# Copying the sinks' columns on ScalarE, and finishing part of the last two rows on ScalarE and GpSimd

## The chip, the core and the metric

The kernel runs on one core of a Trainium2 chip. The core has a matrix engine (TensorE, PE in the profile), a vector engine (VectorE, DVE), a scalar engine (ScalarE, ACT), a general engine (GpSimd, POOL) and a queue that only issues DMAs (SyncE, SP). Each engine works through its own queue in order, and engines wait for each other on semaphores. A DMA that is issued from the queue of ACT or POOL stands in the same line as that engine's computing. The metric is the device time of one execution in microseconds; it was 950.13 us before the change (median of 3 runs, 949.94 to 950.27).

## What is computed

One decoder layer over 1024 tokens and 16 learned meta tokens, width 1024, all in float32:

```
u = rmsnorm(h, g_pre_mix);  q, k, v, xr, yr = split(u @ w_in)
attn = sliding_window_attention_with_sinks(q, k, v, sinks)     # window 128, 8 heads
rec  = gelu(yr) * rg_lru(conv(xr))                             # gated linear recurrence
h = h + rmsnorm(concat(attn, rec) @ w_out, g_post_mix)
f = square(relu(rmsnorm(h, g_pre_ffn) @ w_ff1)) @ w_ff2        # 1024 -> 4096 -> 1024
h = h + rmsnorm(f, g_post_ffn)
```

Two places matter here. In the attention, each head has a sink: a number that takes part in the softmax as one more key, with no value behind it.

```
m = max(max(s), sink);  p = exp(s - m);  denom = sum(p) + exp(sink - m)
```

At the very end, each row of `f` is divided by its root mean square, multiplied by `g_post_ffn`, and added to the residual `h`.

## The kernel before

**Matmuls.** A float32 product is made of three passes in the faster format (`mm3`, L125, L128, L129): each operand is split into a rounded part and a rest (L96 rounds on ACT, L99 takes the rest on DVE), and high by high, high by low and low by high are summed in PSUM. The feed-forward part saves products by sums of blocks, and stores and reloads some of them.

**Order of the work.** The program is written as one stream. A planner gives every instruction a place in its engine's queue, by priority and by a simulated time line of its own; on the chip the queues then run in that fixed order. `behind` (L106) adds an edge that only fixes an order, `lut` (L81) chains ACT's table functions. Buffers come from rings: tag "c" has 8 (L55), the banks of PSUM come in pairs by tag.

**Attention** (`scores`, L566, and `attend`, L620). For 4 pairs of heads and 2 halves of the sequence, `scores` fills two tiles `sn` from ring "c", [128, 4, 257]: two heads by two blocks of 128 queries, 256 keys each, and in column 256 the negated sink. The profile's names of tiles are those of their rings, so `sn` is "c", and its rows are found by line:

- L574, DVE: copies the sinks into column 256 of the four parts, a 128x4 copy; 16 of them in all;
- L590, PE: scores of one head, into a bank "s" of PSUM;
- L596, DVE: takes a bank "s", adds the mask, negates, writes columns 0 to 255, and keeps the minimum in `negm`;
- L604 (in the profile under L82), ACT: exp over columns up to 256, so with the sink, summed into `den`;
- L611, DVE: reciprocal of `den`; L615, POOL: adds the two halves of the keys' columns, 128x512; L616, DVE: divides.

In `attend` PE transposes (L627), ACT and DVE split the result (L96, L99), POOL cuts triangles out of it (L631), PE multiplies with the values (L641), and ACT and DVE take the result out of PSUM (L657, L658). Between them PE works on projections for the next heads and for the recurrence ("fills", with lower priority), which ACT and DVE take out of PSUM too (L117, L118, L451, L453).

**The end.** The second product of the feed-forward part goes in 56 steps. The last of them adds to rows 0 to 511, as four row blocks j = 0 to 3, one after another (L1500). For each, `finish_late` (L1409) adds the last product to the sum (L1415, in the profile under L1012, DVE), squares it with a running sum (L1416 calls L1380, ACT), multiplies by `g_post_ffn` (L1417, under L1012, DVE), takes the root (L1427, under L82, ACT) and the reciprocal `rs` (L1428, DVE). Block 3 comes in two parts of 256 columns for the first 512 columns' steps, so that its second part is short; the other 512 columns were summed earlier (`finish_half`). Then, for the two halves of a row block, columns 512 to 1023 first, one instruction on DVE scales by `rs` and adds the residual `h` (L1430, 128x512), and a DMA writes the half out: the first half from SP's queue, the second from ACT's (L1433). For blocks 0 to 2 these L1430 instructions are put in `held` and ordered behind an instruction of the next block (L1419, L1422), so that DVE takes the next block's sum out of PSUM first. For block 3 L1422 takes one entry of `held` for each of its two parts.

Of the kernel before, what the change touches and what calls it, by code (L numbers as in the profile page):

```python
# [11 lines left out]
AF = mybir.ActivationFunctionType  # L12
ALU = mybir.AluOpType
# [24 lines left out]
def hybrid_layer(  # L38
# [6 lines left out]
    nc = tc.nc  # L45
# [12 lines left out]
    def slot(tag, shape, dt=F32):  # L58
        uid[0] += 1
        return slab.tile(shape, dt, tag=tag, name=f"{tag}{uid[0]}", bufs=bufs[tag])  # L60
# [4 lines left out]
    def bank(tag, shape=(P, 512)):  # L65
        uid[0] += 1
        return ps.tile(list(shape), F32, tag=tag, name=f"ps_{tag}{uid[0]}")
# [13 lines left out]
    def lut(*args, **kwargs):  # L81
        ins = nc.scalar.activation(*args, **kwargs).ins  # L82
        if last_lut[0] is not None:
            tc.add_manual_dep(
                ins, last_lut[0],
                mybir.DependencyInfo(
                    mybir.DependencyClass.NoSync, mybir.DependencyReason.DATA
                ),
                reason="lut",
            )  # L90
        last_lut[0] = ins.name
        return ins
# [13 lines left out]
    def behind(name, *inss):  # L106
        for ins in inss:
            tc.add_manual_dep(
                ins, name,
                mybir.DependencyInfo(  # L110
                    mybir.DependencyClass.NoSync, mybir.DependencyReason.DATA
                ),
                reason="order",
            )
# [434 lines left out]
    for b in range(2):  # L549
        pv = bank("pt", (P, 4, P))  # L550
        for i in range(4):
            o = NMETA + (4 * b + i) * P
# [13 lines left out]
    def scores(j, half, q):  # L566

        g, pairs = j // 2, []
        for bp in range(2):
            sn = slot("c", [P, 4, 257])  # L570
            negm = small.tile([P, 4], F32, name="negm", tag="negm")
            den = small.tile([P, 4], F32, name="den", tag="den")
            rden = small.tile([P, 4], F32, name="rden", tag="rden")
            nc.vector.tensor_copy(  # L574
                sn.rearrange("p (h i) k -> p h i k", h=2)[:, :, :, 256],
                nsink[:, 2 * j : 2 * j + 2].to_broadcast([P, 2, 2]),
            )
            spans = [KEYS if 4 * half + 2 * bp + i else KEYS_0 for i in range(2)]
            if spans[0] is KEYS_0:
                nc.gpsimd.memset(  # L580
                    sn.rearrange("p (h i) k -> p h i k", h=2)[:, :, 0, 0 : P - NMETA], 0.0
                )
            for h in range(2):
                sp_ = bank("s", (P, 2, 256))
                for i, (w0, w1) in enumerate(spans):
                    b = 4 * half + 2 * bp + i
                    c = slice(b * P, (b + 1) * P)
                    o = NMETA + (b - 1) * P
                    for n, k_ in enumerate((khh, kl)):
                        nc.tensor.matmul(  # L590
                            sp_[:, i, w0:w1], q[h][:, c], k_[g][:, o + w0 : o + w1],
                            start=n == 0, stop=n == 1, skip_group_check=True,
                        )
                for i, (w0, w1) in enumerate(spans):
                    k = 2 * h + i
                    top = nc.vector.tensor_tensor_reduce(  # L596
                        out=sn[:, k, w0:w1], in0=sp_[:, i, w0:w1],
                        in1=mask[:, w0:w1], scale=-1.0,
                        scalar=nsink[:, 2 * j + h : 2 * j + h + 1],
                        op0=ALU.add, op1=ALU.min, accum_out=negm[:, k : k + 1],  # L600
                    ).ins
                    if (j, half, bp, k) == (3, 0, 0, 3):
                        behind(top.name, *held_back)
                    power = lut(  # L604
                        sn[:, k, w0:], sn[:, k, w0:], AF.Exp, scale=-1.0,
                        bias=negm[:, k : k + 1], accum_out=den[:, k : k + 1],
                    )
                    if j and half == bp == 0 and k in (0, 2):
                        behind(q_tail[j][0].name, power)
                        behind(q_tail[j][1].name, top)  # L610
            nc.vector.reciprocal(rden, den)  # L611


            one = sn[:, :, 0:P]
            nc.gpsimd.tensor_tensor(one, one, sn[:, :, P:256], op=ALU.add)  # L615
            nc.vector.tensor_tensor(one, one, rden.to_broadcast([P, 4, P]), op=ALU.mult)  # L616
            pairs.append(sn)
        return pairs
# [115 lines left out]
    for j in range(NPAIR):  # L734
        for half in range(2):
            if j % 2 == 0 and half == 0:
                at_pair(j // 2)
            sn = scores(j, half, qs[j])
            with deferred(0 if (j, half) in Q_SLOTS else FILL_LAG):
                next_fill()  # L740
            if (j, half) == (2, 1):
                graw = slot("raw", [P, NLRU, 2, HD])
                for s in range(2):
                    r = HALF[s]
                    for i, w in enumerate((w_x, w_a)):
                        nc.sync.dma_start(
                            graw[r, :, i ^ s, :], w[0, s::2].rearrange("n c d -> c n d")
                        )
                g_all = slot("b", [P, 2, NLRU, 2, HD], F32R)
                gw = g_all[:, 0], g_all[:, 1]  # L750
                with deferred(FILL_LAG):
                    split(*gw, graw)
            if prev is not None:
                attend(*prev)
            prev = (j, half, sn)
# [6 lines left out]
    for s in range(2):  # L762
        for i in range(2):
            nc.vector.tensor_scalar(
                gbias[HALF[i ^ s], s, :], prm[HALF[s], :, 6 - i], 0.5, None,
                op0=ALU.mult,
# [244 lines left out]
    def combine(dst, x0, x1, op):  # L1011
        return nc.vector.tensor_tensor(dst, x0, x1, op=op).ins  # L1012
# [363 lines left out]
    COLS = (slice(0, 512), slice(512, 1024))  # L1376

    def squares(sq, src, n):
        p_ = small.tile([P, 1], F32, name=f"sq{n}", tag=f"sq{n}")
        nc.scalar.activation(sq, src, AF.Square, scale=RMS_SC, accum_out=p_)  # L1380
        return p_
# [11 lines left out]
    halves, held = {}, []  # L1393
# [15 lines left out]
    def finish_late(j, y, parts):  # L1409

        h, o, ssq = halves[j]
        acc = facc["0", j]
        for k, c in enumerate(parts):
            yield k
            last = combine(acc[:, c], y[k], acc[:, c], ALU.add).name  # L1415
            part = squares(y[k], acc[:, c], k)  # L1416
            scaled = combine(o[:, c], acc[:, c], gffn_b[:, c], ALU.mult)  # L1417
            if len(parts) == 1:
                behind(last, *held)  # L1419
                held.clear()  # L1420
            else:
                behind(scaled.name, held.pop(0))  # L1422
            if k < len(parts) - 1:
                nc.vector.tensor_tensor(ssq, ssq, part, op=ALU.add)
        root = small.tile([P, 1], F32, name="root", tag="root")
        rs = small.tile([P, 1], F32, name="rs", tag="rs")
        lut(root, part, AF.Sqrt, bias=ssq)  # L1427
        nc.vector.reciprocal(rs, root)  # L1428
        for c, eng in zip(COLS[::-1], (nc.sync, nc.scalar)):
            held.append(nc.vector.scalar_tensor_tensor(  # L1430
                o[:, c], o[:, c], rs, h[:, c], op0=ALU.mult, op1=ALU.add
            ).ins)
            eng.dma_start(out[j * P : (j + 1) * P, c], o[:, c])  # L1433

    written = set()
# [64 lines left out]
    for j in range(4):  # L1500
        parts = col_parts(6, j)
        for k in finish_late(j, accs[j], parts):
            for n in sorted(ready):
                step_mm(accs[j][k], j, steps[n][1], ready[n], parts[k])
# [31 lines left out]
```

## Time and profile before

| | |
|---|---|
| median of 3 runs | 950.13 us (949.94 to 950.27) |
| the profiled execution's own time | 949.87 us |
| its span, first to last instruction | 947.9 us |
| granted TensorE clock | 0.998 |
| ACT busy | 500.2 us (53%) |
| DVE busy | 679.3 us (72%) |
| POOL busy | 154.7 us (16%) |
| HBM | 115.70 MB read, 23.07 MB written |

How to read the profile's rows. A row of the time line has the start in us from the span's start, the duration in us, engine, line, operation, output and inputs by their rings' names, shape, and a count if several neighbours are merged; in brackets stands the idle time just ahead of it on its engine, and what ended that. Starts and durations of neighbours on one engine overlap a little. A row of the waits names who waited for whom, the sum in us, how often, and the longest. A row of the windows has the stretch, its length, then busy time and count of instructions for PE, its weight loads, DVE, ACT and POOL, then the granted clock, the share of the DMA engines and GB/s. A matmul's shown duration is longer than the distance to the next one, because matmuls are pipelined.

### The profile page before, as it was taken

To read this page: it belongs to the slowest core of one execution; us is meant where nothing else is said; L and a number is where in the kernel's file an instruction comes from. 1 tells how busy PE (TensorE), PEld (TensorE's weight loads), DVE (VectorE), ACT (ScalarE), POOL (GpSimd) and SP (SyncE) were. 2 spreads that over 40 slices of the span, in tenths; PEclk is the share of its full clock that TensorE was granted. 3 is DMA by queue.
4 is the path that set the end of the run, shared out by engine and by line. 5 is a ranking of instruction groups with operands and counts; after the bars stand their busy time and mean duration, and the time that the engine had idled before them with its cause. 6 is when DMAs were issued, how large, how long until landed. Compare 5 with 4: busy or idle time off the path is not lost.

```text
span 947.9 us, 12401 instructions
## 1 busy us (share of the span) xinstructions
PE 938.9 (99%) x4661; PEld 784.7 (83%) x4661; DVE 679.3 (72%) x963; ACT 500.2 (53%) x826; POOL 154.7 (16%) x198
## 2 busy tenths in 40 slices
PE   9999999999999999999999999999999999999997
PEld 8999899878888888888888888888888888888886
DVE  6679898878966786665654566576667676769884
ACT  7556686579345554443655565564533343445451
POOL 2116674600020100000110001101121000003020
PEclk9999999999999999999999999999999999999999
DMA  8221001212245466685655567645677665567412
GB/s 286 53 52 39 23 27 31 89 45 90 80 165 178 134 222 200 201 278 155 222 173 193 156 199 229 204 150 151 155 180 179 181 216 201 175 202 156 115 64 89
DMA packets 85466, 140.62 MB, mean 148 GB/s; under 512 B 5752, under 2 KB 48776, under 8 KB 85408
## 3 DMA queue, kind: packets, MB, share of 16 engines
q1 hardware_dynamic: 74944, 108.39, 35.3%
q0 software_dynamic: 9600, 29.36, 12.1%
q10 hardware_dynamic: 864, 2.10, 0.6%
q8 instruction: 36, 0.59, 0.2%
q14 instruction: 22, 0.18, 0.1%
HBM read 115.70 MB, written 23.07 MB: 146 GB/s over the span
## 4 chain that ended last, share of the span: by engine, by line
PE 97%; DVE 2%; ACT 0%; POOL 0%; issue 0%; DMA 0%; DVEq 0%; ACTq 0%
PE ps_acc L125 12%; PE ps_acc L128 11%; PE ps_acc L129 11%; PE ps_pt L129 7%; PE ps_pt L128 7%; PE ps_pt L125 7%; PE ps_s L125 6%; PE ps_s L129 6%; PE ps_s L128 6%; PE ps_o L125 5%; PE ps_o L129 5%; PE ps_o L128 5%; PE ps_o L641 1%; PE ps_s L590 1%; PE ps_o L986 1%; PE ps_acc L278 1%
## 5 line engine op out<-in xcount | busy, mean ns | idle before, releaser
L96 ACT CAST ws<-raw 128x1024 fp32r<-128x1024 f32 (+1 forms) x64 | 65.4, 1023 | 96.6 <-PE ps_o L128 47.9
L99 DVE TENSOR_TENSOR ws<-raw,ws 128x1024 fp32r<-128x1024 f32 (+1 forms) x65 | 79.0, 1215 | 40.4 <-ACT ws L96 40.4
L125 PE MATMUL ps_acc<-a,ws 128*128 128x256 f32 (+2 forms) x256 | 85.8, 335 | 0.0
L128 PE MATMUL ps_acc<-a,ws 128*128 128x256 f32 (+2 forms) x256 | 84.9, 332 | 0.0
L129 PE MATMUL ps_acc<-a,ws 128*128 128x256 f32 (+2 forms) x256 | 84.7, 332 | 0.0
L96 ACT CAST ws<-e 128x1024 fp32r<-128x1024 f32 x41 | 42.9, 1047 | 65.4 <-PE ps_o L128 38.1
L99 DVE TENSOR_TENSOR b<-b,b 128x1024 fp32r<-128x1024 f32 (+2 forms) x48 | 57.6, 1199 | 27.6 <-PE ps_o L128 22.4
L99 DVE TENSOR_TENSOR ws<-e,ws 128x1024 fp32r<-128x1024 f32 x41 | 50.1, 1223 | 27.1 <-ACT ws L96 27.1
L96 ACT CAST b<-b 128x1024 fp32r<-128x1024 f32 (+2 forms) x48 | 49.4, 1030 | 37.7 <-DVE b L1012 34.6
L631 POOL TENSOR_SCALAR_AFFINE_SELECT c<-c 128x512 fp32r<-128x512 f32 x64 | 54.2, 872 | 30.9 <-ACT c L96 27.2
L178 POOL TENSOR_TENSOR rs<-ms,half_pow 128x1 f32<-128x1 f32 x26 | 19.3, 749 | 204.5 <-DVE ms L174 203.4
L125 PEld LDWEIGHTS ps_acc<-a,ws 128*128 128x128 f32 x256 | 48.2, 188 | 5.4 <-issue 0.6
L129 PEld LDWEIGHTS ps_acc<-a,ws 128*128 128x128 f32 x256 | 48.2, 188 | 4.8
L128 PEld LDWEIGHTS ps_acc<-a,ws 128*128 128x128 f32 x256 | 48.2, 188 | 4.3 <-issue 0.2
L125 PE MATMUL ps_acc<-ws,b 128*128 128x512 f32 (+1 forms) x120 | 46.4, 386 | 0.0
L129 PE MATMUL ps_acc<-ws,b 128*128 128x512 f32 (+1 forms) x120 | 46.2, 385 | 0.0
L128 PE MATMUL ps_acc<-ws,b 128*128 128x512 f32 (+1 forms) x120 | 46.2, 385 | 0.0
L129 PE MATMUL ps_pt<-ws,b 128*128 128x512 f32 x112 | 44.1, 394 | 0.0
L128 PE MATMUL ps_pt<-ws,b 128*128 128x512 f32 x112 | 44.1, 394 | 0.0
L125 PE MATMUL ps_pt<-ws,b 128*128 128x512 f32 x112 | 43.9, 394 | 0.0
L125 PE MATMUL ps_s<-ws,b 128*128 128x512 f32 x110 | 43.3, 395 | 0.0
L128 PE MATMUL ps_s<-ws,b 128*128 128x512 f32 x110 | 43.3, 394 | 0.0
(427 smaller groups left out, 2715.1 us busy)
## 6 DMA issues: line engine op xcount, KB each, us to landing
raw<-in_w_ff_dram SPq DMA_DIRECT2D x51, 512.0 KB, 4.3
e<-in_w_ff_dram SPq DMA_DIRECT2D x33, 512.0 KB, 3.9
m<-in_w_ff_dram SPq DMA_DIRECT2D x16, 512.0 KB, 4.5
raw<-in_w_in_dram SPq DMA_DIRECT2D x12, 512.0 KB, 4.9
d<-in_w_ff_dram SPq DMA_DIRECT2D x12, 512.0 KB, 4.0
s_dram<-d POOLq DMA_DIRECT2D x12, 512.0 KB, 4.0
raw<-in_w_ff_dram POOLq DMA_DIRECT2D x10, 512.0 KB, 5.7
e<-in_w_ff_dram POOLq DMA_DIRECT2D x9, 512.0 KB, 5.7
```

Source lines behind the costliest of these rows:

```text
L96: nc.scalar.copy(hi, src)
L99: low = nc.vector.tensor_tensor(lo, src, f32(hi), op=ALU.subtract).ins
L125: ins = nc.tensor.matmul(dst, lh, rh, start=start, stop=False, skip_group_check=True).ins
L128: nc.tensor.matmul(dst, lh, rl, start=False, stop=False, skip_group_check=True)
L129: last_mm[0] = nc.tensor.matmul(dst, ll, rh, start=False, stop=stop, skip_group_check=True).ins.name
L178: last_pow[0] = nc.gpsimd.tensor_tensor(rs[:n], ms[:n], half_pow[:n], op=ALU.pow).ins.name
L278: last_mm[0] = nc.tensor.matmul(acc[:, :n], w[k // 2][:, kc, :], u[kc][k % 2][:, t0 : t0 + n], start=k == 0 and kc == 0, stop=k == last an ...
L590: nc.tensor.matmul(sp_[:, i, w0:w1], q[h][:, c], k_[g][:, o + w0 : o + w1], start=n == 0, stop=n == 1, skip_group_check=True,)
L631: nc.gpsimd.affine_select(out=m[:, :, side, :], in_=f32(m)[:, :, 1, :], pattern=[[0, 4], [-sign, P]], compare_op=op, fill=0.0, base=0, cha ...
L641: ins = nc.tensor.matmul(po[:, :, oc : oc + size], v, m[:, :, pc : pc + size], start=first and k == 0, stop=last and k == 1, skip_group_ch ...
L986: nc.tensor.transpose(pt[:, i, :], xn[:, kc * P : (kc + 1) * P], ident)
```

## The change

Three edits:

```diff
@@ scores
-            nc.vector.tensor_copy(
+            nc.scalar.copy(
                 sn.rearrange("p (h i) k -> p h i k", h=2)[:, :, :, 256],
                 nsink[:, 2 * j : 2 * j + 2].to_broadcast([P, 2, 2]),
             )
@@ finish_late
             if len(parts) == 1:
                 behind(last, *held)
                 held.clear()
-            else:
+            elif held:
                 behind(scaled.name, held.pop(0))
...
         nc.vector.reciprocal(rs, root)
+        shared = {2: 512, 3: 256}.get(j)
         for c, eng in zip(COLS[::-1], (nc.sync, nc.scalar)):
-            held.append(nc.vector.scalar_tensor_tensor(
-                o[:, c], o[:, c], rs, h[:, c], op0=ALU.mult, op1=ALU.add
-            ).ins)
+            mine = c
+            if shared and c is COLS[0]:
+                s_ = slice(0, shared)
+                nc.scalar.activation(o[:, s_], o[:, s_], AF.Copy, scale=rs)
+                nc.gpsimd.tensor_tensor(o[:, s_], o[:, s_], h[:, s_], op=ALU.add)
+                mine = slice(shared, 512)
+            if mine.start < mine.stop:
+                held.append(nc.vector.scalar_tensor_tensor(
+                    o[:, mine], o[:, mine], rs, h[:, mine], op0=ALU.mult, op1=ALU.add
+                ).ins)
             eng.dma_start(out[j * P : (j + 1) * P, c], o[:, c])
```

The 16 copies of the sinks' columns go from DVE to ACT. Of row block 2, columns 0 to 511 are scaled by ACT and added to the residual by POOL, with nothing left of that half for DVE. Of row block 3, columns 0 to 255 go the same way, and DVE keeps columns 256 to 511. Columns 512 to 1023 of both blocks stay with DVE. `held` then has one entry of block 2, so the second part of block 3 finds it empty. The DMA of the first 512 columns stays on ACT's queue; of block 2 it now waits for POOL, and of block 3 for POOL and DVE.

## The prediction

> **What bounds the kernel now.** I read the page first, then PE's waits, then the stretches of the two places that the change touches.
>
> ```profile
> PE 938.9 (99%) x4661; PEld 784.7 (83%) x4661; DVE 679.3 (72%) x963; ACT 500.2 (53%) x826; POOL 154.7 (16%) x198
> ...
> PE 97%; DVE 2%; ACT 0%; POOL 0%; issue 0%; DMA 0%; DVEq 0%; ACTq 0%
> ```
>
> PE is busy nearly always, and the chain that ended last is 97% PE. So time is saved in two ways only: a gap in PE is closed, or the work behind the last matmul gets shorter. PE's waits, all of them:
>
> ```profile
> PE ps_acc L299 <- POOL b L293: 1.6, 1, 1.6
> PE ps_s L590 <- DVE negm L596: 0.7, 1, 0.7
> PE ps_o L348 <- DVE d L254: 0.3, 1, 0.3
> ```
>
> The first and the third lie in the kernel's first 10 us, and the change doesn't touch them. The second is a score matmul (L590) that waits until DVE has emptied its bank. It is the only gap of the stage with the sinks, and of everything after it. The windows say how full the engines are there:
>
> ```profile
> 61.00:104.00 43.00, 42.26 (x295) 39.10 (x295) 37.37 (x103) 30.95 (x91) 24.99 (x27) 1.00 0.13 38
> 104.00:157.00 53.00, 53.00 (x353) 48.70 (x352) 49.44 (x111) 34.40 (x96) 30.82 (x35) 1.00 0.13 35
> ...
> 941.66:947.93 6.27, 0.00 (x0) 0.00 (x0) 3.00 (x6) 0.80 (x3) 0.00 (x0) 0.72 0.44 167
> ```
>
> DVE is the fullest engine beside PE (37.37 of 43.00 us, 49.44 of 53.00), ACT has a third free. The last row is the end: no matmul, DVE works for 3.00 us, then the last write lands and the program closes.
>
> **The sinks' copies.** What the 16 copies cost now, and where the gap comes from (line 574 as a whole, then DVE, POOL, PE and ACT around the gap):
>
> ```profile
> L574 DVE COPY c<-nsink x16: 155/168/1286, 26.1 to 155.8; 128x4 f32<-128x4 f32 x16
> ...
> 96.09 1.35 DVE L574 COPY c<-nsink 128x4 f32<-128x4 f32 x2
> 97.36 0.17 DVE L611 RECIPROCAL rden<-den 128x4 f32<-128x4 f32 x1
> 97.56 0.43 DVE L658 TENSOR_TENSOR e<-ps_o,e 64x256 f32<-64x256 f32 x1
> 98.02 0.48 DVE L596 CUSTOM_DVE_ANT_0 c<-ps_s,m,nsink 128x256 f32<-128x256 f32 x1
> ...
> 96.12 1.30 POOL L615 TENSOR_TENSOR c<-c 128x512 f32<-128x512 f32 x1
> ...
> 97.83 0.28 PE L128 MATMUL ps_acc<-a,ws 128*128 128x256 f32 x1
> 97.95 0.28 PE L129 MATMUL ps_acc<-a,ws 128*128 128x256 f32 x1
> 98.97 0.51 PE L590 MATMUL ps_s<-b,b 128*128 128x256 f32 x2 [0.74 <-DVE negm L596]
> ...
> 95.98 0.76 ACT L657 COPY e<-ps_o 64x256 f32<-64x256 f32 x2
> 98.02 0.62 ACT L96 CAST b<-e 128x512 fp32r<-128x512 f32 x1 [1.28 <-DVE e L658]
> ```
>
> A copy takes 0.168 us in the median, but one took 1.286. It ended at 97.44, just when POOL's addition that began at 96.12 was over (97.42): the two did not run side by side, DVE stood still for it. Behind it in DVE's queue are L611, L658 and then the two L596 that empty the bank; PE's next score matmul starts at 98.97, 1.02 us after its predecessor, where neighbours are 0.12 apart (97.83, 97.95). So the gap costs **0.90 us**. (The 0.74 in brackets is less, since a matmul's shown end is late.)
>
> Without the copies L611 can start at 96.1. L658 needs ACT's first copy of 95.98, half of 0.76, so it starts at 96.4 and ends at 96.8; the two L596, 0.41 apart, end near 97.7. PE wants the bank at 98.07. The gap is closed with 0.35 us to spare. If ACT puts both new copies ahead of L657, 0.3 to 0.4 us go, and it still closes or nearly so.
>
> What ACT pays: a 128x4 copy is not in the trace for ACT. Nearest are the 128x64 casts and the longer 64x256 copies (0.38):
>
> ```profile
> L96 ACT CAST vm<-ps_o x2: 213/216/220, 59.3 to 59.8; 128x64 fp32r<-128x64 f32 x2
> ```
>
> I take 0.2 us, 16 times 3.2 us, from nothing to 16 x 0.38 = 6.1. In both windows together ACT has 96.00 - 65.35 = 30.65 us free, and this hides it. If it were not hidden, a copy would delay an exp by 0.2 us, and PE only where a bank is already late. The DVE time that comes free beyond this gap buys nothing: PE has no other gap there. Term: **-0.90 us**.
>
> **The end.** DVE, then ACT:
>
> ```profile
> 939.97 0.16 DVE L1428 RECIPROCAL rs<-root 128x1 f32<-128x1 f32 x1
> ...
> 940.49 0.43 DVE L1012 TENSOR_TENSOR a<-a,a 128x256 f32<-128x256 f32 x1
> 940.83 0.75 DVE L1430 SCALAR_TENSOR_TENSOR a<-a,rs,d 128x512 f32<-128x512 f32 x1
> 941.49 0.15 DVE L1424 TENSOR_TENSOR late<-late,sq 128x1 f32<-128x1 f32 x1
> 941.70 0.42 DVE L1012 TENSOR_TENSOR a<-ps_acc,a 128x256 f32<-128x256 f32 x1
> 942.15 0.43 DVE L1012 TENSOR_TENSOR a<-a,a 128x256 f32<-128x256 f32 x1
> 942.50 0.74 DVE L1430 SCALAR_TENSOR_TENSOR a<-a,rs,d 128x512 f32<-128x512 f32 x1
> 943.16 0.15 DVE L1428 RECIPROCAL rs<-root 128x1 f32<-128x1 f32 x1
> 943.35 1.42 DVE L1430 SCALAR_TENSOR_TENSOR a<-a,rs,d 128x512 f32<-128x512 f32 x2
> ...
> 942.15 0.39 ACT L1380 ACTIVATE ps_acc<-a 128x256 f32<-128x256 f32 x1 [1.16 <-DVE a L1012]
> 942.48 0.19 ACT L1380 ACTIVATION_READ_ACCUMULATOR ps_acc<-a 128x1 f32 x1
> 942.70 0.29 ACT L82 ACTIVATE root<-sq,late 128x1 f32<-128x1 f32 x1
> 943.27 1.86 ACTq L1433 DMA_DIRECT2D out_dram<-a  x2
> ```
>
> Now DVE's last instruction ends at 944.77, and the write behind it closes the kernel. Block 2's L1430 at 942.50 goes away; the root is there at 942.99, so the last reciprocal could start at 943.02 in place of 943.16, 0.14 sooner. Then half of the last L1430 goes: 0.43 in place of 0.75.
>
> Against it stands POOL, which must read the same memory as DVE:
>
> ```profile
> 85.92 1.53 DVE L99 TENSOR_TENSOR ws<-raw,ws 128x1024 fp32r<-128x1024 f32 x1
> ...
> 86.34 2.26 POOL L615 TENSOR_TENSOR c<-c 128x512 f32<-128x512 f32 x1
> ...
> 915.36 5.67 POOL L1405 TENSOR_SCALAR late<-late 128x1 f32<-128x1 f32 x1 [7.55 <-ACT a L1402]
> ...
> 915.12 1.22 DVE L99 TENSOR_TENSOR ws<-raw,ws 128x1024 fp32r<-128x1024 f32 x1
> ...
> 919.73 1.22 DVE L99 TENSOR_TENSOR a<-e,a 128x1024 fp32r<-128x1024 f32 x1
> ```
>
> L615 took 2.26 us in place of 1.30 when it met an L99, and ended 1.15 us after that (87.45 to 88.60). A 128x1 instruction of POOL took 5.67 us while DVE ran six with two inputs in SBUF, back to back from 915.12 to 920.95. So the two exclude each other, and a row of DVE instructions can keep POOL out. In the Trainium skill, SBUF — State Buffer, section Who interferes with whom, says the same: a VectorE instruction with two SBUF inputs and a GpSimd instruction that reads SBUF share an interface, and the one that starts second is blocked for the whole of the other. By that rule the end comes out 0.45 us later than if both ran freely, and the rows agree with it.
>
> With exclusion: ACT scales block 2's half from 940.16. The 0.60 us of a 128x512 square is 0.39 at 256 columns, and with a scale from memory 256 columns cost 0.48 (12 of L117):
>
> ```profile
> L117 ACT ACTIVATE a<-ps_o,gcol x12: 468/481/496, 9.5 to 52.2; 128x256 fp32r<-128x256 f32 x9, 128x272 fp32r<-128x272 f32 x3
> ...
> 938.17 0.60 ACT L1380 ACTIVATE ps_pt<-a 128x512 f32<-128x512 f32 x1 [3.04 <-DVE a L1012]
> ```
>
> That gives 0.69 for 512 columns, until 940.85. POOL is kept out by DVE (940.49 to 941.64), then runs its 1.15 beside the sum from PSUM, until 942.8. DVE's product of 942.15 has two inputs in SBUF and waits for that; some 0.1 of its 0.43 are over by then, so it ends at 943.1, and the reciprocal starts near 943.05, 0.1 sooner than now. The last L1430 of columns 512 to 1023 starts 0.19 behind (as 943.16 to 943.35), so 943.24 to 943.99. ACT scales 256 columns until 943.75, and POOL is ready at 943.85 but shut out until 943.99. POOL's 256 columns are not in the trace: between half of 1.15 and 1.30; I take 0.65, since a 128x1 instruction shows a fixed part. With DVE's 0.35 to 0.43 one after the other, in either order, the end is 943.99 + 0.65 + 0.4 = 945.04, against 944.77: about **+0.25 us**. With the dearest POOL (1.30) it is +0.9; with no exclusion the chain is 943.02 + 0.19 + 0.48 + 0.1 + 0.75 = 944.55, **-0.2**.
>
> **Sum.** -0.90 + 0.25 = -0.65 us. The profiled execution took 949.87 (span 947.9, 2 us around it), so 949.2; the median of the runs lies 0.26 above that one, so I forecast **949.5**. A change under 0.2% (1.9 us) is about what a measurement of this kernel can tell from no change.
>
> **Rivals.**
>
> *POOL and DVE run side by side at the end.* -0.90 - 0.2 = -1.1: 949.0. The L615 and L1405 rows speak against it. 10%.
>
> *ACT's queue is late at the end.* Block 2's second DMA stands in ACT's queue and now waits for POOL (942.8). If the planner thinks POOL is done before 942.15 and puts it ahead of the last squares, these wait until 942.8 plus the 0.35 us of an issue (942.85 to 943.2) in place of 942.15, 1.05 later, and root, reciprocal and end follow. Sum 0.25 + 1.05 - 0.90 = +0.4: 950.5. In the trace block 2's DMA stands behind the root (943.27 after 942.70), but there it was ready later, too. 15%.
>
> *The gap only moves.* Another instruction of DVE meets POOL, or L658 is late because the copies stand ahead of L657, and PE loses the same 0.9 elsewhere: +0.25: 950.4. That no other gap is there now speaks against it. 10%.
>
> *Slower: the copies hold ACT.* On ACT a copy that must wait for its buffer of ring "c" (eight, still read by POOL and PE) holds the exps and PSUM evictions queued behind it, and PE runs out of banks. On DVE, nearly always late itself, this wait was over each time; ACT, with a third free, would reach it sooner. A late bank costs about what the one of now costs, 0.9. It decides from three such places: 3 x 0.9 - 0.65 = +2.05; with four it is +2.95: 953.1. Twelve of the 16 copies lie behind 60 us, in seven or so places. ACT's idle stretches (1.28 ahead of 98.02) speak against it. 15%.
>
> *Faster by more than 1.9 us.* PE has nothing left to give but the start; the end would have to lose a microsecond as well, out of the 3.1 between 941.66 and 944.77. Only a planner's order that changes elsewhere could do it. 5%.
>
> My forecast has 45%. Within 0.2% are it and the first three rivals, 80%; slower 15%, faster 5%. The range takes in 949.0 to 950.5 and the bounds of POOL's price and of ACT's copies: 948.6 to 951.2.
>
> **What would show it.** PE's wait L590 <- DVE is gone from the list, and PE's last matmul ends near 940.76. L574 stands on ACT, 16 at 0.2 us. POOL's two additions at the end take 1.3 to 1.9 and 0.8 to 1.2 us from their starts, because of waits; DVE's product on the last part ends together with POOL's first addition plus 0.3. The last matmul to the last ACT DMA issue grows from 3.1 to 3.4 us. I am wrong if PE shows new waits between 60 and 157 us, or ACT's squares wait behind a DMA.

## The result, and the profile after

The changed kernel takes **951.98 us** (median of 11 runs, 951.82 to 954.08; the kernel before on the same chip 950.13). The ratio (of the means) is 1.0023, with a 95% interval of 1.0015 to 1.0031. So the change makes the kernel slower, by 1.85 us in the medians, where 0.6 us faster was forecast, and the time lies above the forecast's range of 948.6 to 951.2. The profiled execution took 951.91 us, with a span of 950.2 us in place of 947.9.

The span is 2.3 us longer, and the traces say in which two places. TensorE's last matmul ends at 942.89 in place of 941.66, 1.23 later, where 0.90 earlier was forecast. From there to the issue of the last DMA (the last L1441 row below; L1430 of before is L1438 in the changed file, L1433 is L1441, and L1434 and L1435 are the new scaling on ACT and addition on POOL) it is now 4.20 us (942.89 to 947.09), against 3.14 before (941.66 to 944.80): 1.06 more, where 0.25 more was forecast. The last issue of before, by itself:

```profile
944.80 0.34 ACTq L1433 DMA_DIRECT2D out_dram<-a  x1
```

First TensorE's waits in the changed kernel, all of them (who waited for whom, sum in us, how often, the longest), and line 574 as a whole:

```profile
PE ps_acc L299 <- POOL b L293: 1.6, 1, 1.6
PE ps_acc L125 <- ACT d L705: 1.6, 1, 1.6
PE ps_o L158 <- DMA vmt<-in_g_pre_ffn_dram: 0.6, 1, 0.6
PE ps_o L348 <- DVE d L254: 0.3, 1, 0.3
...
L574 ACT COPY c<-nsink x16: 183/197/208, 27.5 to 144.4; 128x4 f32<-128x4 f32 x16
```

The wait of L590 for DVE is gone, as forecast. The copies stand on ACT with 0.197 us each. One of the sixteen, at 31.86, came behind 0.43 us in which ACT waited for DVE's L228; ahead of the others the view shows no wait. In place of L590's wait stands a new row: a matmul of L125 waits 1.6 us for ACT's L705. That is a projection for the recurrence, outside the stage that the change touches. The stage with the sinks is now full:

```profile
61.00:104.00 43.00, 43.00 (x299) 39.99 (x299) 37.69 (x106) 32.75 (x98) 26.07 (x28) 1.00 0.13 38
104.00:157.00 53.00, 53.00 (x357) 48.75 (x356) 47.62 (x102) 35.54 (x103) 30.86 (x36) 1.00 0.10 27
```

PE is busy for 43.00 of 43.00 us in place of 42.26, and does 299 matmuls in the first stretch where it did 295. So the gap was closed, and the time was gained there. Counted by the nth matmul to start, the changed kernel is 0.13 us behind the kernel before at 80 us (from the waits of the start), 0.77 ahead at 99 us, so that 0.90 was gained, and 1.33 ahead at 180 us.

**Lost at 180 us.** The time line there, of before (PE, ACT and DVE), and ahead of it the row of who waited for L705's copies, from the view of that line:

```profile
  PEld ps_acc L125: 0.6, 2
...
180.14 0.40 PE L129 MATMUL ps_acc<-a,ws 128*128 128x512 f32 x1
180.52 0.50 PE L125 MATMUL ps_acc<-a,ws 128*128 128x512 f32 x1
...
179.88 0.59 ACT L705 COPY d<-ps_acc 128x512 f32<-128x512 f32 x1 [0.89 <-DVE b L673]
...
178.52 1.33 DVE L673 SCALAR_TENSOR_TENSOR b<-d,prm,b 128x1037 f32<-128x1037 f32 x1
```

And the same instructions in the changed kernel:

```profile
178.81 0.40 PE L129 MATMUL ps_acc<-a,ws 128*128 128x512 f32 x1
180.78 0.50 PE L125 MATMUL ps_acc<-a,ws 128*128 128x512 f32 x1 [1.57 <-ACT d L705]
...
180.15 0.58 ACT L705 COPY d<-ps_acc 128x512 f32<-128x512 f32 x1 [1.53 <-DVE b L673]
...
178.71 1.35 DVE L673 SCALAR_TENSOR_TENSOR b<-d,prm,b 128x1037 f32<-128x1037 f32 x1
```

L705 takes the first projection of the gates' branch out of PSUM into a tile of ring "d". Its tile is the one that the convolution's last step (L673, on DVE) still reads, so L705 waits for that step, and the next L125 waits for L705 to empty the bank. In the kernel before, L673 ended at 179.85, L705 at 180.47, and L125 began at 180.52. That chain was just in time: PE lost 0.15 us there. It had no row among PE's waits: only the spacing of the matmuls (0.38 in place of 0.23) and the 0.6 us that two of PE's weight loads waited show it. In the changed kernel PE is there 1.33 us sooner (178.81 against 180.14), while DVE's convolution is 0.2 us later. So PE stands for 1.57 us, and the lead is gone: by the same count PE is 0.29 behind at 182 us.

**Lost at 195 us.** Here the order of PE's queue is another one. The first gates (L790) are 18 matmuls of 64 rows. Before, they ran together, two at a time, a pair every 0.16 us (first two rows, last two of 18, and the matmul behind them):

```profile
193.64 0.43 PE L790 MATMUL ps_s<-b,b 64*128 64x348 f32 x1
193.65 0.43 PE L790 MATMUL ps_pt<-b,b 64*128 64x348 f32 x1
...
195.02 0.32 PE L790 MATMUL ps_pt<-b,b 64*128 64x344 f32 x1
195.03 0.32 PE L790 MATMUL ps_o<-b,b 64*128 64x344 f32 x1
195.27 0.50 PE L125 MATMUL ps_acc<-a,ws 128*128 128x512 f32 x1
```

In the changed kernel the planner put three matmuls of a projection in between (five L790, one, ten, two, three L790):

```profile
193.28 0.42 PE L790 MATMUL ps_s<-b,b 64*128 64x348 f32 x1
...
193.71 0.32 PE L790 MATMUL ps_pt<-b,b 64*128 64x344 f32 x1
193.96 0.49 PE L125 MATMUL ps_acc<-a,ws 128*128 128x512 f32 x1
194.38 0.42 PE L790 MATMUL ps_s<-b,b 64*128 64x348 f32 x1
...
195.53 0.50 PE L128 MATMUL ps_acc<-a,ws 128*128 128x512 f32 x1
...
196.19 0.73 PE L790 MATMUL ps_o<-b,b 64*128 64x344 f32 x3
196.85 0.50 PE L125 MATMUL ps_acc<-a,ws 128*128 128x512 f32 x1
```

Before, the 18 take 1.63 us (193.64 to 195.27). After, they take 3.57 (193.28 to 196.85), of which the three others are worth 3 x 0.23 = 0.69 at their usual spacing. So 1.25 us are lost where halves stand without a partner and where the form changes (how the loss divides between the two isn't shown), with no gap that a view of waits would list. By the same count the changed kernel is 0.20 behind at 193 us, 1.56 behind at 198, and 1.23 behind at its last matmul.

**Lost at the end.** The changed kernel's end, DVE first, then POOL and ACT:

```profile
942.09 0.74 DVE L1438 SCALAR_TENSOR_TENSOR a<-a,rs,d 128x512 f32<-128x512 f32 x1
942.75 1.22 DVE L1424 TENSOR_TENSOR late<-late,sq 128x1 f32<-128x1 f32 x1
943.89 0.41 DVE L1012 TENSOR_TENSOR a<-ps_acc,a 128x256 f32<-128x256 f32 x1
...
945.21 0.16 DVE L1428 RECIPROCAL rs<-root 128x1 f32<-128x1 f32 x1 [0.44 <-ACT root L82]
945.40 1.61 DVE L1438 SCALAR_TENSOR_TENSOR a<-a,rs,d 128x512 f32<-128x512 f32 x2
...
942.25 1.71 POOL L1435 TENSOR_TENSOR a<-a,d 128x512 f32<-128x512 f32 x1 [19.94 <-ACT a L1434]
945.99 0.75 POOL L1435 TENSOR_TENSOR a<-a,d 128x256 f32<-128x256 f32 x1 [2.04 <-ACT a L1434]
...
941.44 0.72 ACT L1434 ACTIVATE a<-a,rs 128x512 f32<-128x512 f32 x1 [0.90 <-DVE rs L1428]
...
947.09 0.34 ACTq L1441 DMA_DIRECT2D out_dram<-a  x1
```

POOL's addition for block 2 became ready at 942.25, while DVE ran L1438. By the durations it got in when that ended: from 942.83 to its own end at 943.96 are 1.13 us, about the 1.15 that the prediction's L615 took once DVE was done. The next instruction in DVE's queue was the small addition L1424, 128x1: it took 1.22 us in place of 0.15, and ended with POOL's. Behind it in the queue stood the sum out of PSUM (L1012), for which PE had been done since 942.89. It started at 943.89, 1.00 later, where the kernel before took 0.04. Of the 1.06 us, 0.96 are lost here. From this sum to the last reciprocal it is 0.14 less than before (1.32 in place of 1.46), and from there to the last DMA's issue 0.24 more (1.88 in place of 1.64).

### The profile page after: what moved, and what is told of

It reads as the page before. It is cut to its first block, busy times and chain, and to the rows that moved or that the text cites. A ratio compares the mean times of both kernels' runs of the same rounds, so it can differ in the third digit from the quotient of the medians.

```text
span 950.2 us, 12413 instructions
## 1 busy us (share of the span) xinstructions
PE 938.8 (99%) x4661; PEld 785.3 (83%) x4661; DVE 676.5 (71%) x946; ACT 503.2 (53%) x844; POOL 154.4 (16%) x200
## 4 chain that ended last, share of the span: by engine, by line
PE 94%; DVE 4%; ACT 1%; POOL 0%; DMA 0%; issue 0%; DVEq 0%; SPq 0%; ACTq 0%; POOLq 0%
PE ps_acc L125 11%; PE ps_acc L128 11%; PE ps_acc L129 11%; PE ps_pt L129 7%; PE ps_pt L128 7%; PE ps_pt L125 7%; PE ps_s L125 6%; PE ps_s L129 6%; PE ps_s L128 6%; PE ps_o L125 5%; PE ps_o L129 5%; PE ps_o L128 5%; PE ps_o L641 1%; PE ps_s L590 1%; PE ps_o L986 1%; PE ps_acc L278 1%
## 5 line engine op out<-in xcount | busy, mean ns | idle before, releaser
L125 PE MATMUL ps_acc<-a,ws 128*128 128x256 f32 (+2 forms) x256 | 85.9, 336 | 1.6 <-ACT d L705 1.6
L128 PE MATMUL ps_acc<-a,ws 128*128 128x256 f32 (+2 forms) x256 | 85.6, 334 | 0.0
L631 POOL TENSOR_SCALAR_AFFINE_SELECT c<-c 128x512 fp32r<-128x512 f32 x64 | 51.4, 826 | 32.2 <-ACT c L96 23.9
L125 PEld LDWEIGHTS ps_acc<-a,ws 128*128 128x128 f32 x256 | 48.3, 189 | 7.1 <-ACT d L705 2.0
L128 PEld LDWEIGHTS ps_acc<-a,ws 128*128 128x128 f32 x256 | 48.2, 188 | 4.5 <-issue 0.4
L125 PE MATMUL ps_acc<-ws,b 128*128 128x512 f32 (+1 forms) x120 | 46.4, 386 | 0.0
L128 PE MATMUL ps_acc<-ws,b 128*128 128x512 f32 (+1 forms) x120 | 46.1, 384 | 0.0
L128 PE MATMUL ps_pt<-ws,b 128*128 128x512 f32 x112 | 44.2, 395 | 0.0
L125 PE MATMUL ps_pt<-ws,b 128*128 128x512 f32 x112 | 44.0, 395 | 0.0
L125 PE MATMUL ps_s<-ws,b 128*128 128x512 f32 x110 | 43.4, 396 | 0.0
L128 PE MATMUL ps_s<-ws,b 128*128 128x512 f32 x110 | 43.3, 394 | 0.0
```

The lines of the kernel that those rows point to most:

```text
L125: ins = nc.tensor.matmul(dst, lh, rh, start=start, stop=False, skip_group_check=True).ins
L128: nc.tensor.matmul(dst, lh, rl, start=False, stop=False, skip_group_check=True)
L631: nc.gpsimd.affine_select(out=m[:, :, side, :], in_=f32(m)[:, :, 1, :], pattern=[[0, 4], [-sign, P]], compare_op=op, fill=0.0, base=0, cha ...
```

## The experiments

My theory after these traces: three separate losses. The planner's new order cuts the first gates (1.25 us); L705's wait for ring "d" takes the lead that the copies bring (1.6 us); and POOL's addition holds DVE's L1424 and with it the last sum (1.06 us). The first rival: the copies on ACT cost time by themselves, because they hold ACT's other work. The second: the end is longer because DVE's and POOL's last instructions go one after the other, whatever POOL's first addition does.

Each kernel ran 10 or 11 times beside the kernel before, whose median was 950.04 to 950.17 in those rounds. The last two columns are from the trace of one execution.

| kernel | median us | ratio to before (95%) | last matmul ends | from there to the last DMA's issue |
|---|---|---|---|---|
| before | 950.13 | 1 | 941.66 | 3.14 |
| the change | 951.98 | 1.0023 (1.0015 to 1.0031) | 942.89 | 4.20 |
| e1_sinks | 950.98 | 1.0011 (1.0002 to 1.0019) | 942.47 | 3.14 |
| e2_tail | 951.01 | 1.0007 (0.9998 to 1.0016) | 941.70 | 4.18 |
| e7_copies_pool | 950.75 | 1.0009 (1.0000 to 1.0018) | 942.70 | 3.14 |
| e5_sinks_gates | 949.68 | 0.9996 (0.9987 to 1.0004) | 941.66 | 3.14 |
| e6_sinks_gates_y | 947.81 | 0.9977 (0.9968 to 0.9986) | 939.71 | 3.14 |
| e10_before_gates_y | 949.04 | 0.9990 (0.9981 to 0.9998) | 940.84 | 3.14 |
| e3_tail_sum_act | 950.41 | 1.0004 (0.9994 to 1.0013) | 941.80 | 3.67 |
| e9_tail_sum_act_sp | 951.00 | 1.0013 (1.0004 to 1.0021) | 942.88 | 3.25 |
| e4_block3 | 950.23 | 1.0005 (0.9996 to 1.0014) | 941.51 | 3.45 |
| e11_after_gates_y | 949.21 | 0.9990 (0.9981 to 0.9999) | 939.74 | 4.17 |

Two things about this table. The intervals of e2_tail, e5_sinks_gates, e3_tail_sum_act and e4_block3 take in 1, and that of e7_copies_pool begins there: their times alone hardly tell them from the kernel before, and what is said of them rests on their traces. And each trace has its own start: at 26 us PE is anywhere from 0.34 us ahead of before (e4_block3) to 1.24 behind (e9_tail_sum_act_sp). Counted from 80 us to the last matmul, PE loses 1.10 us against before in the change and the same 1.10 in e1_sinks, and 0.97 in e7_copies_pool; it gains 0.17 in e5_sinks_gates, 1.82 in e6_sinks_gates_y and in e11_after_gates_y, and 0.91 in e10_before_gates_y.

### e1_sinks: the copies on ACT alone

```diff
-            nc.vector.tensor_copy(
+            nc.scalar.copy(
                 sn.rearrange("p (h i) k -> p h i k", h=2)[:, :, :, 256],
```

Expected: 

> Only the sinks' copies go to ScalarE; the end is that of before. Theory: the queue orders up to the last rows are those of the changed kernel, so PE's last matmul ends 1.2 us later than before (near 942.9), with the gap of 1.6 us ahead of L125 that waits for ScalarE's L705, and with the gates' 18 matmuls (L790) cut into pieces; the end takes 3.1 us from the last matmul to the last write's issue, as before. 951.3 us. Rival (all of the loss is in the end): 950.1 or less.

It took 950.98, 0.3 under what I had expected. The gap at 99 us is gone, the wait for L705 is there with 1.57 us at 180.4, the first gates are cut in the same way, and the end is that of before. The first edit alone loses 0.8 us on PE's time line (942.47 against 941.66; I had expected 942.9). The difference to the change is the start, where this trace is 0.42 us ahead of that of the change at 80 us; from there on both lose 1.10. The two losses of the middle belong to it, none to the tail's edits.

### e2_tail: the last two rows alone

```diff
+        shared = {2: 512, 3: 256}.get(j)
...
+            if shared and c is COLS[0]:
+                s_ = slice(0, shared)
+                nc.scalar.activation(o[:, s_], o[:, s_], AF.Copy, scale=rs)
+                nc.gpsimd.tensor_tensor(o[:, s_], o[:, s_], h[:, s_], op=ALU.add)
+                mine = slice(shared, 512)
```

Expected: 

> Only the end's edits; the sinks' copies stay on VectorE. Theory: PE's last matmul ends where it did (941.7), with the gap of 0.74 us at 98; GpSimd's addition for block 2 shuts out the 128x1 addition L1424 for about 1 us, the sum of PSUM behind it starts 1 us after the last matmul, and the last write is issued 4.2 us behind the last matmul in place of 3.1: 951.2 us. Rival (the end costs nothing, all is lost in the sinks' stage): 950.1.

It took 951.01. One wait of PE and two rows of DVE at the end of this kernel:

```profile
PE ps_s L590 <- DVE negm L596: 0.7, 1, 0.7
...
941.53 1.22 DVE L1424 TENSOR_TENSOR late<-late,sq 128x1 f32<-128x1 f32 x1
942.67 0.41 DVE L1012 TENSOR_TENSOR a<-ps_acc,a 128x256 f32<-128x256 f32 x1
```

PE's time line is that of before, with its gap of 0.7 us. The end is the change's end: L1424 takes 1.22 us again, and the sum starts 0.97 after the last matmul's end (941.70 to 942.67). So the two losses add up without touching each other: 0.85 and 0.88 us in the medians, 1.85 together in the change.

### e7_copies_pool: the copies on GpSimd

```diff
-            nc.vector.tensor_copy(
+            nc.gpsimd.tensor_copy(
                 sn.rearrange("p (h i) k -> p h i k", h=2)[:, :, :, 256],
```

Expected: 

> The sinks' copies on GpSimd in place of ScalarE, everything else as before. Theory (the loss is in the planner's order, which has the gates cut as in e1_sinks, and in the wait for L705; ScalarE's own 3.2 us cost nothing): the gap of 0.74 us at 99 is gone and the stage's lead and losses are those of e1_sinks: 950.7 to 951.2. Rival (ScalarE's copies cost the time): 949.0 to 949.5.

It took 950.75. Here ACT does nothing more than before, and still PE waits for L705:

```profile
PE ps_acc L125 <- ACT d L705: 1.0, 1, 1.0
```

The first gates are cut in the same way. The wait is shorter here because PE comes with a smaller lead, 1.16 at 180 us in place of 1.74 in e1_sinks. So the first rival falls: what ACT pays for the copies is not the cause. What is common to both kernels is that the copies leave DVE, that PE comes earlier, and that the planner, on another time line, orders the gates in another way.

### e5_sinks_gates: the first gates kept together

```diff
             if (c, t0) == (0, 696):
-                behind(ins.name, begun[1][KC + 2])
+                behind(ins.name, begun[1][KC + 2], begun[2][5])
```

This is e1_sinks with one more edge that only fixes the order: the matmuls that were put in between now come behind the last of the first gates' 18.

Expected: 

> The sinks' copies on ScalarE, end as before, and an order edge that puts the sixth group of a fill (begun[2][5]) behind the first gates' last matmul, so that these 18 matmuls stand together again. Theory (planner's order): PE's last matmul ends 1.2 us sooner than with the sinks' copies alone, near 941.7, while the wait for L705 stays: 950.1. Rival (the 16 copies hold ScalarE, and PE with it): as with the sinks' copies alone, 951.3.

It took 949.68, 1.30 less than e1_sinks. From 180 to 260 us e1_sinks loses 2.89 us against before, this kernel 1.63, so 1.26 come back with the gates, as much as the rows above showed lost. PE's last matmul ends only 0.81 earlier, since this trace is 0.46 behind that of e1_sinks at 80 us. The wait for L705 stays, with 1.6 us. The kernel is back at the time of before: with the gates repaired, the copies gain a lead and the wait at 180 us takes it away.

### e6_sinks_gates_y: and the first chunk's output from another ring

```diff
         def run(w):
-            y = slot("b" if c == 1 else "d", [P, T])
+            y = slot("b" if c < 2 else "d", [P, T])
```

With this, L705 writes to a tile of ring "b", and needn't wait for the convolution.

Expected: 

> As e5_sinks_gates, and the first y tile (fill_y(0)) takes its buffer from ring b, so that ScalarE's L705 no longer waits for the buffer that VectorE's last convolution step (L673) still reads. Theory (PE's lead of 1.3 us is lost at that wait): the gap of 1.6 us at 180 goes and PE's last matmul ends 1.0 to 1.3 us sooner than in e5: 948.4 to 948.7. Rival (the lead is lost to VectorE as a whole, so that it waits elsewhere a little later): PE's lead is gone by 210 us all the same, 949.7.

It took **947.81**: faster than both kernels, by 2.2 us against before. All of PE's waits in this kernel:

```profile
PE ps_acc L299 <- POOL b L293: 1.6, 1, 1.6
PE ps_o L641 <- POOL c L631: 0.2, 1, 0.2
```

The wait for L705 is gone, and so is the one of L590. PE is 1.88 us ahead of before at 185 us and still 1.47 ahead at 210, so the rival, a lead that is gone by then all the same, falls. Not all of it stays: 0.90 are left at 215 us. Among the 18 matmuls of a later gate one of a projection now stands (L128 at 211.67), and a good half us is lost there. Against e5_sinks_gates the kernel takes 1.87 us less, and the wait was 1.6; it gained more than I had expected, and the next kernel shows where.

### e10_before_gates_y: the two edits of the order without the copies

The kernel before with the two edits of e5 and e6, and the copies left on DVE.

Expected: 

> The kernel before, with two edits of the order alone: the eighteen matmuls of the first gates are kept ahead of the fills that the planner would put between them, and the first chunk's output tile comes from the buffers b instead of d. The sinks' copies stay on VectorE and the end is that of before. Theory (the copies on ScalarE close a gap of 0.8 us near 98 us of TensorE's time-line and hand on a lead of 1.3 to 2 us, and these two edits only keep that lead from being lost at 180 and 195 us): the gap near 98 us stays, TensorE had no wait at 180 us in the kernel before, so this kernel takes 949.6 to 950.1. Rival (the two edits are a gain by themselves, and the copies bring nothing): 947.6 to 948.4, as the kernel with the copies and both edits took.

It took 949.04. My expectation was wrong: the two edits gain about 1.1 us by themselves in the medians, and 0.82 by the end of PE's last matmul. Its gap at 99 us is there, as expected:

```profile
PE ps_s L590 <- DVE negm L596: 0.8, 1, 0.8
```

At 215 us this kernel's PE is 0.30 us behind before, with the same cut in the later gate as in e6_sinks_gates_y. The gain comes later and evenly: between 440 and 870 us it gets 1.26 us ahead, with the same order of matmuls, no single step of over 50 ns, and a granted clock of 1.00 in both kernels. e6_sinks_gates_y and e11_after_gates_y gain 1.06 there, e5_sinks_gates, e1_sinks and the change only 0.26 to 0.27. So it comes with the other ring for y, in a stretch where y is long done. What makes matmuls there 0.3% quicker I have not found; the tiles' places in memory are an argument, not a result.

What the copies are worth with both edits is the difference between this kernel and e6_sinks_gates_y: 940.84 - 939.71 = 1.13 us on the time line, and 1.23 us by the medians. Of the 1.13, 0.22 stand between the two traces at 80 us, ahead of the gap; from there on it is 0.91.

### e3_tail_sum_act: the small addition on ACT

```diff
-                nc.vector.tensor_tensor(ssq, ssq, part, op=ALU.add)
+                nc.scalar.activation(ssq, part, AF.Identity, bias=ssq)
```

This is e2_tail with L1424 taken out of DVE's queue, so that POOL can't hold it there.

Expected: 

> The end's edits alone, with the 128x1 addition L1424 taken off VectorE (ScalarE adds it as the bias of an Identity). Theory (GpSimd's addition shuts VectorE's L1424 out, and the PSUM sum queues behind it): the PSUM sum starts right behind the last matmul again, only the product behind it meets GpSimd, and the last write is issued 3.2 to 3.5 us behind the last matmul: 950.2 to 950.5, 0.7 to 1.0 under the end's edits as they are. Rival (ScalarE's scaling holds up its squares and root): no faster than the end's edits as they are, 951.2, or slower by ScalarE's further 0.3.

It took 950.41, 0.6 less than e2_tail. Two rows of DVE and two of ACT:

```profile
941.84 0.42 DVE L1012 TENSOR_TENSOR a<-ps_acc,a 128x256 f32<-128x256 f32 x1
942.29 0.83 DVE L1012 TENSOR_TENSOR a<-a,a 128x256 f32<-128x256 f32 x1
...
942.87 0.34 ACTq L1441 DMA_DIRECT2D out_dram<-a  x1
943.25 0.29 ACT L82 ACTIVATE root<-sq,late 128x1 f32<-128x1 f32 x1 [0.45 <-POOL a L1435]
```

Now the sum starts right behind the last matmul (941.84 after 941.80), although POOL is at work: reading from PSUM it is not held. The product of 942.29, with both inputs in SBUF, is held (0.83 in place of 0.42). That is the order of things that the prediction had assumed. But the end, with 3.67 us, is above the 3.2 to 3.5 that I had expected and 0.53 longer than before, because the root now stands in ACT's queue behind block 2's DMA, which waits for POOL.

### e9_tail_sum_act_sp: and block 2's DMA on SP's queue

```diff
-        for c, eng in zip(COLS[::-1], (nc.sync, nc.scalar)):
+        for c, eng in zip(COLS[::-1], (nc.sync, nc.sync if j == 2 else nc.scalar)):
```

Expected: 

> As e3_tail_sum_act, with the DMA of block 2's first half on SyncE's queue in place of ScalarE's. Theory (in e3 ScalarE's root stood 0.45 us behind this DMA, which waits for GpSimd): the root follows the squares at once, the last write is issued 3.2 to 3.3 us behind the last matmul in place of 3.67: 950.0 to 950.1. Rival (VectorE's product behind GpSimd's addition ends later than the root anyway): 3.5 or more, 950.3.

The end is 3.25 us, 0.42 less than in e3_tail_sum_act, as expected: the root no longer waits for the DMA. But the whole took 951.00, above what I had expected, and not because of the end. In its trace PE's last matmul is 1.2 us late, and that comes from the kernel's first 25 us:

```profile
PE ps_s L278 <- DVE ws L339: 1.0, 1, 1.0
...
23.98 0.17 DVE L503 TENSOR_SCALAR nsink<-nsink 128x8 f32<-128x8 f32 x1 [2.17 <-DMA nsink<-in_attn_sinks_dram]
```

DVE waits for the load of the sinks at the very start, until 23.98; in the kernel before the same L503 began at 22.16. Nothing in this edit touches that load; its DMA was issued at 12.97 and took 11.0 us to land, before it was 12.23 and 9.9. The trace is that of an execution of 951.68 us, and the eleven lie between 950.28 and 952.64. So this kernel's time doesn't tell what the end is worth; its trace does.

### e4_block3: only the quarter of the last row

```diff
-        shared = {2: 512, 3: 256}.get(j)
+        shared = {3: 256}.get(j)
```

Expected: 

> The end's edits for block 3 alone (256 columns to ScalarE and GpSimd, block 2 stays on VectorE), the sinks' copies on VectorE. Theory (the loss is block 2's addition meeting L1424, block 3's quarter only brings GpSimd and VectorE one behind the other): the PSUM sum starts right behind the last matmul, the last reciprocal where it was, GpSimd's 0.75 and VectorE's rest follow each other: last write's issue 3.2 to 3.4 us behind the last matmul, 950.1 to 950.4. Rival (the quarter is shared without cost): 2.9 us, 949.9.

It took 950.23, and its end is 3.45 us, 0.31 longer than before and a little above the 3.2 to 3.4 that I had expected.

```profile
943.21 1.15 DVE L1438 SCALAR_TENSOR_TENSOR a<-a,rs,d 128x512 f32<-128x512 f32 x2
...
943.52 0.51 ACT L1434 ACTIVATE a<-a,rs 128x256 f32<-128x256 f32 x1 [0.67 <-DVE rs L1428]
...
944.11 0.83 POOL L1435 TENSOR_TENSOR a<-a,d 128x256 f32<-128x256 f32 x1 [23.23 <-ACT a L1434]
```

DVE's two instructions are over at 944.36, but ACT's scaling of 0.51 and POOL's addition of 0.83, one after the other, end at 944.94. In the kernel before DVE's two whole halves took 1.42. So even with block 2 left alone, the quarter on two other engines ends later than DVE alone would.

### e11_after_gates_y: the whole change with both edits of the order

Expected: 

> The whole change, with both edits of the order (the first gates' eighteen matmuls kept together, the first chunk's output tile from the buffers b). Theory (the sinks' part and the tail's part add up): 947.81 of the kernel with the sinks' part and both edits, plus 1.05 for the longer way from the last matmul to the last transfer's issue (4.2 us instead of 3.14), so 948.9, range 948.4 to 949.4, and TensorE's last matmul ends at 939.5 to 940.2. Rival (the end's length depends on what TensorE leaves late, so the tail's loss goes with it): 947.8 to 948.2.

It took 949.21. The end is 4.17 us, and PE's last matmul ends at 939.74, as in e6_sinks_gates_y. So 1.4 us of e6's gain are given away at the end, by the medians, and 1.03 by the trace. The parts add up, and the end's loss is the same when PE is done 3 us sooner.

## Why the prediction was wrong, point by point

- **What bounds the kernel (PE, and the work behind its last matmul): right.** All of the difference lies in these two.
- **The sinks' gap: right.** The wait of L590 is gone, L611 runs without POOL in its way, the copies take 0.197 us where 0.2 was forecast, and ACT's free time hides them. From 80 to 99 us the change gains 0.90 us, as forecast, and where the lead can pass, 0.91 of it are there at the end (e6_sinks_gates_y against e10_before_gates_y, from 80 us on). That it comes out so close to the forecast is in part luck: on the way the difference of these two traces is anywhere from 0.9 to 1.5 us.
- **That a closed gap reaches the end: wrong, and this is the step that failed first.** The prediction said that PE has no other gap, and took the lead of 98 us to be kept for the 840 us behind it. It isn't kept: at 180 us PE meets a chain (L673, L705, L125) that had no slack before, stands for 1.57 us, and is 0.29 behind where it had been 1.33 ahead. The list of PE's waits shows only what is late now, not what is just in time. The rival "the gap only moves" was of this kind, with the price right (the lead is lost), but with the wrong reason against it, that no other gap is there now.
- **That the rest of the order stays: wrong.** The planner's order came up once, as a way in which the kernel might become faster by over 1.9 us, at 5%. It came out on the other side: 1.25 us for the first gates. With both, the first edit costs 0.8 us (1.10 counted from 80 us on) where 0.9 gain was forecast.
- **The slower rival, copies that hold ACT: fell.** It had the sign and, by luck, about the time, but not the cause: one copy alone was held, for 0.43 us, with no wait of PE behind it, and e7_copies_pool loses nearly the same without ACT (0.97 against 1.10 from 80 us on).
- **The end: the exclusion was right, its place wrong.** The prediction let POOL in at 941.64, behind L1424, so that it would hold the product alone, beside the sum from PSUM. POOL got in one instruction earlier, ahead of L1424, and so held the sum too. e3_tail_sum_act, where L1424 is out of the way, has the order as forecast: product 0.83, and 3.25 us with the DMA out of the way as well (e9_tail_sum_act_sp), against 3.14 + 0.25 = 3.39 forecast. The rows of before did speak for it: POOL was ready while DVE's L1430 ran, the prediction had ACT done at 940.85 and L1430 from 940.83 to 941.58, and it took from the L1405 row that back-to-back instructions keep POOL out.
- **The rival that ACT's queue is late: right in its mechanism, without effect in the change.** Where the sum comes in time, the root (not the squares, which the prediction named) does wait behind block 2's DMA (e3_tail_sum_act); in the change all of it is late already.
- **The last stretch, DVE and POOL one after the other: right.** From DVE's start to its last end it took 1.61 us (945.40 to 947.01); forecast were 1.80. So the second rival of the experiments is true only of this part. By itself it brings nothing against the 1.42 us that DVE took alone, as e4_block3 shows as well.

In the sum: on PE's side +1.23 in place of -0.90 (0.13 of it from the start), at the end +1.06 in place of +0.25.

## What to carry to other kernels

Before you count a closed gap as a gain, follow the lead to the next chain that the engine meets, and look there for links that end just in time: a wait of the weight loads, or a spacing that is a little too wide, is a sign of a chain with no slack. Where a planner orders the queues, a moved instruction can change the order far away, so compare the queues' orders outside the touched stage before you believe a local sum. And work given to a second engine at the end pays only if that engine's reads don't exclude the first one's: with block 2's half and the quarter of block 3, every variant here ended later than DVE alone.

## What the runs showed of the hardware that I had not expected

- Between two DVE instructions that follow each other, a waiting POOL instruction can get in, and then holds even a 128x1 addition for 1.07 us (1.22 in place of 0.15), three times over (the change, e2_tail, e11_after_gates_y). In the Trainium skill, SBUF — State Buffer, section Who interferes with whom, whichever of the two issues first holds the shared ports for its whole instruction, and the other is fully blocked. This trace agrees for both turns: POOL's addition took 1.71 us from 942.25 because DVE's L1438 was there first, and L1424 ended at 943.97 with POOL's 943.96. Why POOL got in at once here, and was kept out by six DVE instructions in the L1405 row of before, stays open. The same section says that a VectorE instruction with at most one SBUF input, outside its two-port modes, doesn't contend with GpSimd; the trace agrees: with one input in PSUM, DVE's L1012 ran beside POOL at its usual 0.42 us (e3_tail_sum_act).
- Matmuls of 64 rows ran two at a time, a pair every 0.16 us. Three full-height matmuls put among 18 of them cost 1.25 us beyond their own time, and one put among 18 of a later gate 0.53 (e10_before_gates_y: 2.40 us in place of 1.64, less its own 0.23).
- The load of the sinks let DVE's L503 begin at 22.16 us in one kernel's trace and at 23.98 in another's, with nothing changed on its way; 1.2 us of that were still there at the end.
- An even stretch of matmuls, with the same order and no waits, ran 0.3% quicker (1.26 us in 430) when an early tile came from another ring, at a granted clock of 1.00 both times. What makes it so stays open.
